# Elementwise arithmetic taken from GpSimd to VectorE and ScalarE in a two-layer attention, RWKV and experts trunk

## The chip, the cores and the metric

The kernel runs on one core of one Trainium2 chip. Such a core has a matrix engine (TensorE, PE in the profile; its weight loads are PEld), VectorE (DVE), ScalarE (ACT), GpSimd (POOL) and a queue that only issues transfers (SyncE, SP). Each engine takes its instructions strictly in the order in which they stand in its own queue. The metric is the time of one execution on the device in microseconds.

## The reference

Two layers over 1024 tokens of width 1024. The parts that the change touches are the projection, the RWKV half, the attention half and the output projection:

```python
for l in range(2):
    sh1, sc1, gt1, sh2, sc2, gt2 = split(silu(c) @ ada_w[l] + ada_b[l], 6)
    h = rms_norm(x, norm1_g[l]) * (1 + sc1) + sh1
    proj = h @ w_in[l]                                  # 1024 x 3232
    q, k, v = proj[:, :1536]                            # 4 heads, 2 maps of 64 each
    attn = diff_attention(rotary(q), rotary(k), v)      # softmax1 - lambda * softmax2, chunk mask
    p = proj[:, 1536:]; p = p + (shift(p) - p) * mu     # RWKV-7: 8 heads of 64
    r, k, v, w_lo, a_lo, g_lo = split(p)
    decay, a, g = exp(-exp(w)), sigmoid(a0 + a_lo @ a_up), sigmoid(g_lo) @ g_up
    kk = normalise(k * k_k); kf = k * (1 + (a - 1) * k_a)
    y = scan: S = S * w_t + (S a_t) b_t + v_t k_t;  y_t = S r_t
    rwkv = (head_group_norm(y) * lnx_g + lnx_b + sum(r * kf * r_k) * v) * g
    x = x + gt1 * (concat(attn, rwkv) @ w_out[l])
    h2 = rms_norm(x, norm2_g[l]) * (1 + sc2) + sh2
    x = x + gt2 * experts(h2)                           # 32 experts, top group, top 2
out = rms_norm(x, final_g)
```

All is float32. A product that must keep float32 accuracy is made of three faster ones: each factor is split into a high part (rounded to the matrix engine's narrower format, `fp32r`) and a low part, the difference between the value and its high part.

## The kernel before

Per layer there are three stages: the first norm (`norm1`), `phase_a` (projection, RWKV, attention, most of the output projection), and routing with the experts (`moe`).

**The weights of the input projection** come in 25 column blocks of 128 per layer. `split_w` (line 339) loads one (`wa_raw`), makes `wa_hi` by a copy (L346, on ScalarE but for the first two of a layer) and `wa_lo` by a subtraction (L347). There are two buffers each of hi and lo, so that a new `wa_hi` can be written only when the matrix engine is through with the block before last. `proj_cm` (L359 to L361) multiplies hi by hi, lo by hi and hi by lo.

**RWKV** goes by four pairs of heads (`hp`) and four quarters of the sequence (`q`), 256 tokens each. `rwkv_first` is called for each pair: `begin` makes two small products and their tanh (L641, L642), `chain` (lines 645 to 671) makes from them in some 13 VectorE instructions the tiles `arv`, `bk` and `bkb`; `bkb` is `bk` times `pend`, the decay at each chunk's end, and `arv[:, 0]` is a diagonal of `pend`. `products` multiplies them (`aa`) and masks them (`z`, L685), `turn` transposes `arv` and `bkb` on the matrix engine. The results go through memory in `sp_z` and `sp_av`. `solve` (L748, L750) inverts small triangles in 62 VectorE instructions for each pair.

`rwkv_second` takes these up again in 16 units of 256 tokens a layer: `rwkv_front` and `rwkv_mid` are products with small copies; `rwkv_back` carries the state from chunk to chunk: a product `rb_s` (L893), an addition on VectorE into `b_sb` (L895), and the next product that waits for it. Beside it stands the bonus `b_bo` (L879), a product of the read-out with one number per head; every second unit ends in `rwkv_last`, the norm of the read-out (L921 to L933) and the gate (L940).

**Attention** loads for each of 4 heads the two maps of keys and queries (`load_head`), makes hi by a ScalarE copy (L1091, L1096) and lo by a subtraction (L1092, L1097); the scores (L1171 to L1174), their maximum (L1176), the exponential (L1178), the difference of the two maps (L1185 to L1187), a transposition (L1196, L1197) and the product with the values (L1205) follow. `out_weights` makes hi and lo of the 8 blocks of the output projection (L1232 to L1234).

**The order.** `phase_a` is written as generators that `weave` interleaves by hand-set costs and lags. After that the framework's scheduler orders each engine's queue once more by its own estimate of times, so the place of an instruction in its queue moves with every change of engine.

Of the kernel before, what the change touches and what calls it, by code (L numbers as in the profile page):

```python
# [10 lines left out]
F32 = mybir.dt.float32  # L11
# [41 lines left out]
class Trunk:  # L53
# [285 lines left out]
    def split_w(self, wp, l, i, eng=None):  # L339

        nc = self.nc
        raw = wp.tile([128, NK, 128], F32, name="wa_raw", tag="wa_raw", bufs=1)
        nc.sync.dma_start(raw, self.a["w_in"][l, i])
        hi = wp.tile([128, NK, 128], F32R, name="wa_hi", tag="wa_hi")
        lo = wp.tile([128, NK, 128], F32R, name="wa_lo", tag="wa_lo")
        (eng or nc.vector.tensor_copy)(hi, raw)  # L346
        nc.gpsimd.tensor_tensor(lo, raw, hi.bitcast(F32), op=OP.subtract)  # L347
        return hi, lo


# [270 lines left out]
    def rwkv_first(self, hp, rp, ep, psum, krv, l2, w_up, a_up, sp):  # L621
# [22 lines left out]
        def chain(q):  # L644
            k, r, v = (x[:, H * q:H * q + H] for x in krv)
            kk = self.kn[:, H * q:H * q + H]
            th, ta = st["th"], st["ta"]
            P, u, rk = tl("P"), tl("u"), tl("rk")
            arv, bkb, bk = tl("arv", [128, 4, 4, 64]), tl("bkb", [128, 2, 4, 64]), tl("bk", [128, 2, 4, 64])
            nc.vector.tensor_scalar(th, th, 1.0, None, op0=OP.add)  # L650
            nc.vector.tensor_tensor_scan(u, self.smul, th, 0.0, op0=OP.mult, op1=OP.add)
            nc.scalar.activation(P, u, AF.Exp, scale=-0.5 * DECAY)
            nc.scalar.activation(u, u, AF.Exp, scale=0.5 * DECAY)

            nc.vector.tensor_scalar(ta, ta, -0.5, -0.5, op0=OP.mult, op1=OP.add)
            nc.vector.tensor_scalar(th, ta, self.nka[:, hp:hp + 1], self.omka[:, hp:hp + 1], op0=OP.mult, op1=OP.add)
            nc.vector.tensor_mul(th, th, k)
            nc.vector.tensor_mul(ta, ta, kk)
            nc.vector.scalar_tensor_tensor(rk, r, self.r_k[:, hp:hp + 1], th, op0=OP.mult, op1=OP.mult)
            kk3, P3 = v3(kk), v3(P)  # L660
            pend = P3[:, :, 63:64]
            nc.vector.tensor_mul(arv[:, 2, :, 1:64], kk3[:, :, 1:64], P3[:, :, 0:63])
            nc.scalar.copy(arv[:, 2, :, 0:1], kk3[:, :, 0:1])
            nc.vector.tensor_mul(arv[:, 1], v3(r), P3)
            nc.vector.tensor_mul(bk[:, 0], v3(ta), v3(u))
            nc.vector.tensor_mul(bk[:, 1], v3(th), v3(u))
            nc.scalar.copy(arv[:, 3], v3(v))
            for j in range(2):
                nc.gpsimd.tensor_tensor(bkb[:, j], bk[:, j], pend.to_broadcast([128, 4, 64]), op=OP.mult)
            nc.gpsimd.tensor_tensor(arv[:, 0], self.id2[:, None, :].to_broadcast([128, 4, 64]), pend.to_broadcast([128, 4, 64]), op=OP.mult)  # L670
            return arv, bkb, bk, rk

        def products(q, bk, arv, z):
# [190 lines left out]
    def rwkv_back(self, hp, q, t, pool, psum):  # L864
# [10 lines left out]
        if r == 0:  # L875
            self.bo = pool.tile([128, 4, 128], F32, name="b_bo", tag="b_bo")
            self.yh = pool.tile([128, 4, 128], F32, name="b_y", tag="b_y", bufs=2)
        bs = self.bsum[:, hp, 2 * q:2 * q + 2].rearrange("p t h -> p (t h)").unsqueeze(2).to_broadcast([128, 4, 64])
        nc.gpsimd.tensor_tensor(self.bo[:, r:r + 2].rearrange("p t (h n) -> p (t h) n", h=2), e[:, 1].rearrange("p t (h n) -> p (t h) n", h=2),  # L879
                                bs, op=OP.mult)  # L880
        hs = [slice(64 * h, 64 * h + 64) for h in range(2)]
        first = 0
# [33 lines left out]
    def rwkv_last(self, hp, half, y, bo, pool, psum):  # L916

        nc = self.nc
        y3 = y.rearrange("p t (h n) -> p (t h) n", h=2)
        st = pool.tile([128, 8, 2], F32, name="b_st", tag="b_st")  # L920
        nc.vector.tensor_reduce(st[:, :, 0:1], y3, axis=AX.X, op=OP.add)  # L921
        nc.vector.tensor_scalar(st[:, :, 0:1], st[:, :, 0:1], -1.0 / 64, None, op0=OP.mult)
        nc.vector.tensor_tensor(y3, y3, st[:, :, 0:1].to_broadcast([128, 8, 64]), op=OP.add)
        sq = pool.tile([128, 8, 64], F32, name="b_sq", tag="b_sq")
        nc.scalar.activation(sq, y3, AF.Square)
        nc.vector.tensor_reduce(st[:, :, 1:2], sq, axis=AX.X, op=OP.add)
        rs = self.rsqrt(pool, st[:, :, 1], 8, GN_EPS, 1.0 / 64, "gn")
        nc.vector.tensor_tensor(y3, y3, rs.unsqueeze(2).to_broadcast([128, 8, 64]), op=OP.mult)
        cs = slice(128 * hp, 128 * hp + 128)
        lnx = self.lnx  # L930
        nc.gpsimd.tensor_tensor(y, y, lnx[:, 0].unsqueeze(1).to_broadcast([128, 4, 128]), op=OP.mult)
        nc.gpsimd.tensor_tensor(bo, bo, lnx[:, 1].unsqueeze(1).to_broadcast([128, 4, 128]), op=OP.add)
        nc.gpsimd.tensor_tensor(y, y, bo, op=OP.add)  # L933

        def gate():
            ps = psum.tile([128, 4, 128], F32, name="rb_gt", tag="rb")
            for i in range(4):
                tl = 4 * half + i
                nc.tensor.matmul(ps[:, i, :], self.sg[0:96, 128 * tl:128 * tl + 128], self.g_up[0:96, cs], start=True, stop=True)
            nc.vector.tensor_mul(y, y, ps)  # L940
            nc.sync.dma_start(self.ad[half][:, :, 512 + 128 * hp:640 + 128 * hp], y)
            yield 0.85, 0.0

        self.add(3, gate(), self.clock + 12.0)
# [128 lines left out]
    def load_head(self, h):  # L1073


        nc, stage = self.nc, self.stage
        keep = self.stk[max(h - 1, 0)]
        qs, ks, kl = [], [], []
        halves = [slice(0, 64), slice(64, 128)]

        def tile(n, dt=F32R):
            return keep.tile([128, T], dt, name=f"at_{n}", tag=f"at_{n}")


        for j, m, x in ((1, 0, tile("q0", F32)), (1, 1, tile("q1", F32)), (0, 0, tile("v", F32)), (0, 1, stage.tile([128, T], F32, name="st", tag="st"))):
            for r in halves:
                nc.sync.dma_start(x[r], self.heads[h, j][halves[m]])
            if j:
                ks.append(tile(f"k{m}"))
                kl.append(tile(f"l{m}"))  # L1090
                nc.scalar.copy(ks[m], x)  # L1091
                nc.gpsimd.tensor_tensor(kl[m], x, ks[m].bitcast(F32), op=OP.subtract)  # L1092
            else:
                dst = tile(f"q{m}")
                qs.append(dst)
                nc.scalar.copy(dst, x)  # L1096
                nc.gpsimd.tensor_tensor(dst[64:128], x[64:128], dst[64:128].bitcast(F32), op=OP.subtract)  # L1097
        v = tile("v", F32).rearrange("p (t n) -> p t n", n=128)
        self.stacks[h] = (qs, ks, kl, v)
        nc.sync.dma_start(v, self.heads[h, 2])  # L1100
# [119 lines left out]
    def out_weights(self, l, k, wp, gate, keep):  # L1220
# [10 lines left out]
                      for n in names[2 * k:2 * k + 2])  # L1231
        nc.vector.tensor_tensor(raw, raw, gate, op=OP.mult)  # L1232
        nc.scalar.copy(hi, raw)
        nc.gpsimd.tensor_tensor(lo, raw, hi.bitcast(F32), op=OP.subtract)  # L1234
        self.wo[k] = hi, lo

    def open_output(self, l, x_src, side):
# [736 lines left out]
```

## Time and profile before

| | |
|---|---|
| median of 3 runs | 2728.67 us (2727.2 to 2737.83) |
| the profiled execution | 2742.43 us |
| its span | 2740.6 us |
| mean granted TensorE clock | 0.912 of full speed |
| GpSimd, busy | 711.9 us (26%), 525 instructions |
| VectorE, busy | 1836.7 us (67%) |
| ScalarE, busy | 1131.5 us (41%) |
| TensorE, busy | 2400.2 us (88%) |

Busy time of the matrix engine is modelled and contains waiting in its own pipe, so 88% is not 88% of its peak. In the span the first layer's first norm and its weights take up to about 150 us, its RWKV products to 450, the state's units beside the heads' projections to 760, attention with the output projection to 1000, the routing and experts to 1390; the second layer has the same stages from 1390, 1500, 1850, 2050 and 2300 us on.

### The profile page before, as it was taken

What the parts mean: (1) busy time and instruction counts of PE and PEld (TensorE: products, weight loads), DVE (VectorE), ACT (ScalarE), POOL (GpSimd) and SP (SyncE); (2) the same over time, 40 slices, a digit from 0 to 9 for tenths busy, and PEclk for the clock granted to TensorE, in tenths of its full rate; (3) what the DMA queues carried; (4) which work ended last, traced back from release to release, by engine and by line L of the source; (5) the groups of instructions that cost most, each with busy time, mean ns of one, the idle gap of its engine ahead of it and who ended that gap; (6) DMA issues with size and microseconds to landing.
All of it is one profiled execution on the core that took longest, in us unless ns stands there. A gap on an engine that the chain in (4) does not pass through costs nothing. (4 is left out here: it accounts for less than half of the span.)

```text
span 2740.6 us, 45306 instructions
## 1 busy us (share of the span) xinstructions
PE 2400.2 (88%) x17313; PEld 1836.5 (67%) x17313; DVE 1836.7 (67%) x3803; ACT 1131.5 (41%) x2020; POOL 711.9 (26%) x525
## 2 busy tenths in 40 slices
PE   5998989898979969999959888889986897999992
PEld 3676657687767866777737666667765786677771
DVE  3358875464658477877753689974648847787775
ACT  4333332244345225555544333324426422455552
POOL 4122221313141013333311222323314200233330
PEclk7999988798979979999979989889988897999996
DMA  8476675534272258999851434355426224899985
GB/s 286 159 233 222 177 218 155 155 115 132 88 218 70 96 193 303 355 336 368 309 213 47 155 107 150 113 153 156 136 76 204 73 89 180 303 384 352 335 311 200
DMA packets 262787, 542.68 MB, mean 198 GB/s; under 512 B 76376, under 2 KB 180768, under 8 KB 232608
## 3 DMA queue, kind: packets, MB, share of 16 engines
q1 hardware_dynamic: 234560, 484.61, 52.6%
q0 software_dynamic: 23376, 40.99, 4.0%
q10 hardware_dynamic: 4624, 14.06, 1.4%
q8 instruction: 142, 2.33, 0.4%
q14 instruction: 85, 0.70, 0.1%
HBM read 459.29 MB, written 120.09 MB: 211 GB/s over the span
## 5 line engine op out<-in xcount | busy, mean ns | idle before, releaser
L1618 DVE TENSOR_TENSOR w_lo<-w_gu,w_hi 128x2048 fp32r<-128x2048 f32 x134 | 306.4, 2287 | 69.1 <-ACT w_hi L1617 68.8
L1617 ACT CAST w_hi<-w_gu 128x2048 fp32r<-128x2048 f32 x134 | 255.7, 1908 | 211.0 <-PE h_ps L1670 204.3
L359 PE MATMUL pj<-hh,wa_hi 128*128 128x512 f32 x800 | 338.2, 423 | 2.1 <-DVE bsum L711 0.7
L361 PE MATMUL pj<-hh,wa_lo 128*128 128x512 f32 x800 | 328.1, 411 | 4.3 <-POOL wa_lo L347 4.3
L360 PE MATMUL pj<-hl,wa_hi 128*128 128x512 f32 x800 | 329.7, 412 | 1.2 <-DVE hl L336 1.1
L1698 POOL DMA_INDIRECT yd<-yo,idx_s x70 | 183.5, 2621 | 289.9 <-DVE yo L1695 275.1
L1709 PE MATMUL y_ps<-w_d,hT 128*128 128x512 f32 x560 | 252.3, 593 | 3.4 <-ACTq L1770 2.4
L1669 PE MATMUL h_ps<-w_hi,xT_hi 128*128 128x512 f32 x560 | 243.0, 434 | 4.4 <-ACT xT_hi L1653 4.4
L1670 PE MATMUL h_ps<-w_hi,xT_lo 128*128 128x512 f32 x560 | 222.5, 397 | 2.5 <-DVE xT_lo L1654 2.5
L1671 PE MATMUL h_ps<-w_lo,xT_hi 128*128 128x512 f32 x560 | 222.4, 397 | 0.0
L347 POOL TENSOR_TENSOR wa_lo<-wa_raw,wa_hi 128x1024 fp32r<-128x1024 f32 x50 | 123.4, 2468 | 296.2 <-ACT wa_hi L346 235.3
L359 PEld LDWEIGHTS pj<-hh,wa_hi 128*128 128x128 f32 x800 | 156.2, 195 | 42.9 <-issue 7.5
L361 PEld LDWEIGHTS pj<-hh,wa_lo 128*128 128x128 f32 x800 | 155.9, 195 | 41.1 <-POOL wa_lo L347 5.7
L360 PEld LDWEIGHTS pj<-hl,wa_hi 128*128 128x128 f32 x800 | 156.0, 195 | 37.1 <-DVE hl L336 4.4
L1709 PEld LDWEIGHTS y_ps<-w_d,hT 128*128 128x128 f32 x560 | 100.9, 190 | 104.8 <-issue 100.4
L1637 POOL DMA_INDIRECT xg<-h2d,idx_g x70 | 75.8, 1082 | 232.8 <-PE xT_ps L1645 204.2
L1669 PEld LDWEIGHTS h_ps<-w_hi,xT_hi 128*128 128x128 f32 x560 | 107.3, 192 | 38.0 <-issue 11.5
L1670 PEld LDWEIGHTS h_ps<-w_hi,xT_lo 128*128 128x128 f32 x560 | 107.3, 192 | 36.6 <-DVE th L1661 11.5
L1654 DVE TENSOR_TENSOR xT_lo<-xT_ps,xT_hi 128x1024 fp32r<-128x1024 f32 x70 | 85.7, 1225 | 65.6 <-ACT xT_hi L1653 65.6
L1671 PEld LDWEIGHTS h_ps<-w_lo,xT_hi 128*128 128x128 f32 x560 | 106.9, 191 | 23.0
L1178 ACT ACTIVATE at_p<-at_s,at_mx 128x256 f32<-128x256 f32 (+7 forms) x128 | 95.0, 743 | 64.4 <-DVE at_mx L1176 63.8
L748 DVE TENSOR_TENSOR sv_m<-sv_t,sv_n 64x31 f32<-64x31 f32 (+15 forms) x248 | 103.1, 416 | 26.4 <-DMA sv_n<-sp_z 21.8
(436 smaller groups left out, 5227.3 us busy)
## 6 DMA issues: line engine op xcount, KB each, us to landing
w_gu<-in_moe_w_gu SPq DMA_DIRECT2D x140, 1024.0 KB
w_d<-in_moe_w_down SPq DMA_DIRECT2D x70, 1024.0 KB
ada_w<-in_ada_w SPq DMA_DIRECT2D x80, 512.0 KB
wa_raw<-in_w_in SPq DMA_DIRECT2D x50, 512.0 KB
sp_z<-z SPq DMA_DIRECT2D x32, 768.0 KB
b_zz<-sp_z SPq DMA_DIRECT2D x32, 512.0 KB
cy<-yd SPq DMA_DIRECT2D x16, 1024.0 KB
qkv<-qst SPq DMA_DIRECT2D x48, 256.0 KB
```

The costliest lines, as they stand in the source:

```text
L347: nc.gpsimd.tensor_tensor(lo, raw, hi.bitcast(F32), op=OP.subtract)
L359: nc.tensor.matmul(ps, hi[:, k, :], self.hh[k][:, sl], start=(k == 0), stop=False)
L360: nc.tensor.matmul(ps, hi[:, k, :], self.hl[k][:, sl], start=False, stop=False)
L361: nc.tensor.matmul(ps, lo[:, k, :], self.hh[k][:, sl], start=False, stop=(k == NK - 1))
L748: eng.tensor_tensor(t3, tt[:, 0:j + 1, j].unsqueeze(2).to_broadcast([64, j + 1, 31 - j]), nt[:, j, j + 1:32].unsqueeze(1).to_broadcast([64 ...
L1617: self.nc.scalar.copy(hi, raw)
L1618: eng.tensor_tensor(lo, raw, hi.bitcast(F32), op=OP.subtract)
L1669: nc.tensor.matmul(ph, hi[:, k, :], whi[:, k % 4, :], start=(k == 0), stop=False)
L1670: nc.tensor.matmul(ph, lo[:, k, :], whi[:, k % 4, :], start=False, stop=False)
L1671: nc.tensor.matmul(ph, hi[:, k, :], wlo[:, k % 4, :], start=False, stop=(k == NK - 1))
L1698: st = nc.gpsimd.indirect_dma_start(out=self.yd, out_offset=bass.IndirectOffsetOnAxis(ap=self.idx_s[:, e:e + 1], axis=0), in_=yos[e % 2], ...
L1709: nc.tensor.matmul(po[:, 512 * half:512 * half + 512], hT[:, k, :], w[:, k, 512 * half:512 * half + 512], start=(k == 0), stop=(k == 1))
```

## The change

All tensor arithmetic that GpSimd does between the first norm and the experts is given to other engines. The subtractions L347, L1092, L1097 and L1234, the bonus L879 and the three operations of the read-out's norm (L931 to L933) go to VectorE with the same operands. The two products `bkb` and the diagonal `arv[:, 0]` (three instructions of 256 elements a partition for each quarter) become eight ScalarE copies with a scale taken from one column of `pend`: four of 128 elements and four of 64. GpSimd keeps its memory fills, its number patterns and the transfers it issues.

```diff
@@ split_w
-        nc.gpsimd.tensor_tensor(lo, raw, hi.bitcast(F32), op=OP.subtract)
+        nc.vector.tensor_tensor(lo, raw, hi.bitcast(F32), op=OP.subtract)
@@ rwkv_first, chain
-            for j in range(2):
-                nc.gpsimd.tensor_tensor(bkb[:, j], bk[:, j], pend.to_broadcast([128, 4, 64]), op=OP.mult)
-            nc.gpsimd.tensor_tensor(arv[:, 0], self.id2[:, None, :].to_broadcast([128, 4, 64]), pend.to_broadcast([128, 4, 64]), op=OP.mult)
+            for i in range(4):
+                nc.scalar.activation(bkb[:, :, i], bk[:, :, i], AF.Copy, scale=pend[:, i])
+            for i in range(4):
+                nc.scalar.activation(arv[:, 0, i], self.id2, AF.Copy, scale=pend[:, i])
@@ rwkv_back
-        nc.gpsimd.tensor_tensor(self.bo[:, r:r + 2]..., e[:, 1]..., bs, op=OP.mult)
+        nc.vector.tensor_tensor(self.bo[:, r:r + 2]..., e[:, 1]..., bs, op=OP.mult)
@@ rwkv_last
-        nc.gpsimd.tensor_tensor(y, y, lnx[:, 0]..., op=OP.mult)
-        nc.gpsimd.tensor_tensor(bo, bo, lnx[:, 1]..., op=OP.add)
-        nc.gpsimd.tensor_tensor(y, y, bo, op=OP.add)
+        nc.vector.tensor_tensor(y, y, lnx[:, 0]..., op=OP.mult)
+        nc.vector.tensor_tensor(bo, bo, lnx[:, 1]..., op=OP.add)
+        nc.vector.tensor_tensor(y, y, bo, op=OP.add)
@@ load_head
-                nc.gpsimd.tensor_tensor(kl[m], x, ks[m].bitcast(F32), op=OP.subtract)
+                nc.vector.tensor_tensor(kl[m], x, ks[m].bitcast(F32), op=OP.subtract)
-                nc.gpsimd.tensor_tensor(dst[64:128], x[64:128], dst[64:128].bitcast(F32), op=OP.subtract)
+                nc.vector.tensor_tensor(dst[64:128], x[64:128], dst[64:128].bitcast(F32), op=OP.subtract)
@@ out_weights
-        nc.gpsimd.tensor_tensor(lo, raw, hi.bitcast(F32), op=OP.subtract)
+        nc.vector.tensor_tensor(lo, raw, hi.bitcast(F32), op=OP.subtract)
```

The changed kernel has one line more in `chain`, so a line after it is numbered one higher (L895 is L896 there).

The queues move as follows. The first place is ScalarE's queue in the first layer's RWKV products, from one quarter's transposed tile `avt` to the next quarter's exponentials `P` and `u`; before:

```order
L693 COPY avt<-tp 128x512
L663 COPY arv<-kn 128x4
L667 COPY arv<-krv 128x256
L693 COPY z<-tp 128x512
L641 ACTIVATE th<-zwa,hbias_338 128x256
L642 ACTIVATE ta<-zwa,hbias_338 128x256
L652 ACTIVATE P<-u 128x256
L653 ACTIVATE u<-u 128x256
```

and in the changed kernel:

```order
L694 COPY avt<-tp 128x512
L663 COPY arv<-kn 128x4
L667 COPY arv<-krv 128x256
L671 ACTIVATE arv<-id_93,P 128x64 x4
L694 COPY z<-tp 128x512
L669 ACTIVATE bkb<-bk,P 128x2x64 x4
L641 ACTIVATE th<-zwa,hbias_338 128x256
L642 ACTIVATE ta<-zwa,hbias_338 128x256
L346 CAST wa_hi<-wa_raw 128x1024
L652 ACTIVATE P<-u 128x256
L653 ACTIVATE u<-u 128x256
```

The four copies of `bkb` now stand in front of the next quarter's tanh (L641), and those of the diagonal in front of the transposed `z`.

The second place is VectorE's queue in the same stage of the changed kernel, where `chain` (`th`, `ta`, `arv`, `bk`) and `solve` (`sv_m`, `sv_t`) are interleaved:

```order
L656 TENSOR_SCALAR th<-ta,ka_340 128x256
L749 TENSOR_TENSOR sv_m<-sv_t,sv_n 64x135
L347 TENSOR_TENSOR wa_lo<-wa_raw,wa_hi 128x1024
L657 TENSOR_TENSOR th<-th,krv 128x256
L658 TENSOR_TENSOR ta<-ta,kn 128x256
L751 TENSOR_TENSOR sv_t<-sv_t,sv_m 64x5x27
L377 SCALAR_TENSOR_TENSOR krv<-pj,pv_334,krv 128x511
L662 TENSOR_TENSOR arv<-kn,P 128x4x63
```

A weight's low part stands in the middle of a chain there, behind which the chain's other instructions have to wait for `wa_hi` too; before, that subtraction was in GpSimd's queue.

The third place is VectorE's queue where the state's units run (`b_sb`) and the first head's tiles for attention are made; before:

```order
L928 TENSOR_TENSOR b_y<-b_y,rs_y_gn 128x512
L821 COPY b_tt<-rb_t 32x4x32
L895 TENSOR_TENSOR b_sb<-rb_s,b_gg 64x64 x4
L838 COPY b_w<-rb_w 128x256
L895 TENSOR_TENSOR b_sb<-rb_s,b_gg 64x64 x2
```

and in the changed kernel:

```order
L929 TENSOR_TENSOR b_y<-b_y,rs_y_gn 128x512
L822 COPY b_tt<-rb_t 32x4x32
L932 TENSOR_TENSOR b_y<-b_y,b_lnx 128x512
L934 TENSOR_TENSOR b_y<-b_y,b_bo 128x512
L880 TENSOR_TENSOR b_bo<-b_e,bsum 128x256 x2
L933 TENSOR_TENSOR b_bo<-b_bo,b_lnx 128x512
L1093 TENSOR_TENSOR at_l_5728<-at_q_5721,at_k_5727 128x1024
L896 TENSOR_TENSOR b_sb<-rb_s,b_gg 64x64 x2
L1093 TENSOR_TENSOR at_l_5734<-at_q_5722,at_k_5733 128x1024
L896 TENSOR_TENSOR b_sb<-rb_s,b_gg 64x64 x2
L839 COPY b_w<-rb_w 128x256
L347 TENSOR_TENSOR wa_lo<-wa_raw,wa_hi 128x1024
```

Six moved instructions stand in front of a pair of state additions that followed at once before, and one more between that pair and the next.

## Rows read from the trace of the kernel before

**Rows 1.** Busy time by stage: span, PE, PEld, DVE, ACT, POOL (instructions), clock, DMA, GB/s.

```profile
150.00:450.00 300.00, 272.12 (x2345) 198.26 (x2346) 214.99 (x538) 98.98 (x200) 76.34 (x81) 0.91 0.69 212
450.00:760.00 310.00, 279.27 (x3301) 229.37 (x3300) 178.18 (x559) 108.32 (x280) 69.95 (x53) 0.88 0.41 119
760.00:1000.00 240.00, 210.94 (x1190) 179.55 (x1188) 163.26 (x383) 107.96 (x252) 46.82 (x28) 0.89 0.42 138
1500.00:1850.00 350.00, 306.15 (x2659) 235.45 (x2658) 278.91 (x740) 122.48 (x265) 90.00 (x81) 0.91 0.43 134
1850.00:2050.00 200.00, 185.60 (x2105) 151.25 (x2104) 98.85 (x312) 74.97 (x185) 56.68 (x40) 0.95 0.42 122
2050.00:2300.00 250.00, 209.83 (x1196) 179.50 (x1195) 176.39 (x396) 118.69 (x288) 46.17 (x26) 0.91 0.39 129
```

**Rows 2.** Timeline, one meeting of both engines: start us, us, engine, line, form.

```profile
372.80 2.95 POOL L347 TENSOR_TENSOR wa_lo<-wa_raw,wa_hi 128x1024 fp32r<-128x1024 f32 x1 [7.75 <-ACT wa_hi L346]
373.46 2.52 DVE L748 TENSOR_TENSOR sv_m<-sv_t,sv_n 64x220 f32<-64x220 f32 x1
376.78 0.37 DVE L750 TENSOR_TENSOR sv_t<-sv_t,sv_m 64x220 f32<-64x220 f32 x1
```

**Rows 3.** Timeline of DVE: the first and the last held instruction, with a neighbour.

```profile
34.98 2.34 DVE L108 TENSOR_TENSOR rs_u_n<-rs_u_n,rs_y_n 128x2 f32<-128x2 f32 x1
37.36 0.16 DVE L109 SCALAR_TENSOR_TENSOR rs_y_n<-rs_u_n,rs_y_n 128x2 f32<-128x2 f32 x1
...
2173.55 2.22 DVE L1212 SCALAR_TENSOR_TENSOR at_ob<-at_ob,rs_y_sub,subg 128x128 f32<-128x128 f32 x1
```

**Rows 4.** Timeline of PE: two waits, [idle us before, and what ended it].

```profile
239.23 1.14 PE L681 MATMUL aa<-arv,bk 64*64 64x128 f32 x14 [2.72 <-DVE arv L664]
...
2178.27 0.65 PE L1171 MATMUL at_s<-at_k,at_q 128*128 128x512 f32 x1 [2.49 <-ACT at_p L1178]
```

**Rows 5.** Groups of POOL, by form: count, busy us, mean ns, idle before, releasers.

```profile
L347 POOL TENSOR_TENSOR wa_lo<-wa_raw,wa_hi 128x1024 fp32r<-128x1024 f32 x50 | 123.4, 2468 | 296.2 <-ACT wa_hi L346 235.3 <-DVE sv_t L750 23.4 <-DVE rs_u_n L107 20.9
L669 POOL TENSOR_TENSOR bkb<-bk,P 128x256 f32<-128x256 f32 x64 | 44.7, 717 | 30.1 <-PE tp L692 14.4 <-DVE bk L666 11.9 <-DVE bk L665 2.8
L1092 POOL TENSOR_TENSOR at_l<-at_q,at_k 128x1024 fp32r<-128x1024 f32 x16 | 38.9, 2433 | 56.2 <-ACT at_k L1091 56.2
L670 POOL TENSOR_TENSOR arv<-id,P 128x256 f32<-128x256 f32 x32 | 28.6, 892 | 233.8 <-PE tp L692 138.1 <-ACT P L652 38.6 <-DVE sv_t L750 18.4
L931 POOL TENSOR_TENSOR b_y<-b_y,b_lnx 128x512 f32<-128x512 f32 x16 | 20.9, 1308 | 287.2 <-issue 182.1 <-DVE b_y L928 92.7 <-PE pj L360 9.1
```

**Rows 6.** Groups of DVE, by form: operations of the moved shapes.

```profile
L1791 DVE TENSOR_TENSOR cy<-cy 128x1024 f32<-128x1024 f32 x16 | 19.4, 1221 | 17.0 <-DMA cy<-yd 16.9
L665 DVE TENSOR_TENSOR bk<-ta,u 128x256 f32<-128x256 f32 x32 | 14.1, 441 | 0.2
L923 DVE TENSOR_TENSOR b_y<-b_y,b_st 128x512 f32<-128x512 f32 x16 | 11.1, 691 | 0.5
```

**Rows 7.** L347 alone in the two RWKV product stages: span, POOL busy (count), clock, DMA.

```profile
150.00:450.00 300.00, 28.42 (x12) 0.91 0.69 212
1500.00:1850.00 350.00, 34.38 (x13) 0.91 0.43 134
```

**Rows 8.** Waits over the whole span: who waited for whom, us, times, longest.

```profile
ACT wa_hi L346 <- PE pj L360: 93.0, 29, 9.3
POOL at_l L1092 <- ACT at_k L1091: 56.2, 10, 20.5
PE pj L361 <- POOL wa_lo L347: 4.3, 4, 1.5
```

**Rows 9.** Groups of ACT, by form: copies without and with a scale of one column.

```profile
L346 ACT CAST wa_hi<-wa_raw 128x1024 fp32r<-128x1024 f32 x46 | 48.1, 1047 | 106.8 <-PE pj L360 93.0 <-issue 7.1 <-DMA wa_raw<-in_w_in 3.7
L667 ACT COPY arv<-krv 128x256 f32<-128x256 f32 x32 | 13.1, 409 | 2.0 <-DVE krv L377 2.0
L323 ACT ACTIVATE n_y<-x,rs_y_n 128x1024 f32<-128x1024 f32 x8 | 8.7, 1139 | 0.6 <-DVE rs_y_n L109 0.6
L663 ACT COPY arv<-kn 128x4 f32<-128x4 f32 x32 | 6.5, 202 | 0.1
```

More of the change, by code (lines that the diff above doesn't have):

```diff
@@ L878, in rwkv_back @@
         bs = self.bsum[:, hp, 2 * q:2 * q + 2].rearrange("p t h -> p (t h)").unsqueeze(2).to_broadcast([128, 4, 64])
-        nc.gpsimd.tensor_tensor(self.bo[:, r:r + 2].rearrange("p t (h n) -> p (t h) n", h=2), e[:, 1].rearrange("p t (h n) -> p (t h) n", h=2),
+        nc.vector.tensor_tensor(self.bo[:, r:r + 2].rearrange("p t (h n) -> p (t h) n", h=2), e[:, 1].rearrange("p t (h n) -> p (t h) n", h=2),
                                 bs, op=OP.mult)
@@ L930, in rwkv_last @@
         lnx = self.lnx
-        nc.gpsimd.tensor_tensor(y, y, lnx[:, 0].unsqueeze(1).to_broadcast([128, 4, 128]), op=OP.mult)
-        nc.gpsimd.tensor_tensor(bo, bo, lnx[:, 1].unsqueeze(1).to_broadcast([128, 4, 128]), op=OP.add)
-        nc.gpsimd.tensor_tensor(y, y, bo, op=OP.add)
+        nc.vector.tensor_tensor(y, y, lnx[:, 0].unsqueeze(1).to_broadcast([128, 4, 128]), op=OP.mult)
+        nc.vector.tensor_tensor(bo, bo, lnx[:, 1].unsqueeze(1).to_broadcast([128, 4, 128]), op=OP.add)
+        nc.vector.tensor_tensor(y, y, bo, op=OP.add)
         def gate():
```

## The prediction

> **What bounds the kernel now.** I read the busy time by stage first, because the change leaves the experts alone: nothing moves in the two expert stages, about 390 and 440 us, and all of it lies in the six stages of [rows 1]. There the reader should compare the engines within a row. In the RWKV products (150 to 450 and 1500 to 1850 us) VectorE is busy for 215 of 300 and 279 of 350 us, 76% together, the fullest engine after a matrix engine whose busy time is modelled; ScalarE has 33 and 35%. Where the state's units run (450 to 760, 1850 to 2050) VectorE has 277 of 510 us, 54%; in attention (760 to 1000, 2050 to 2300) 340 of 490, 69%. So a VectorE instruction is dear in the first kind of stage and cheap in the second.
>
> Next I looked in the timeline for VectorE instructions that take far longer than their form. In [rows 2] one of 220 elements on 64 partitions takes 2.52 us, while the next of the same size takes 0.37. It starts 0.66 us after a GpSimd subtraction and ends 0.23 us after it (372.80 + 2.95 = 375.75; 373.46 + 2.52 = 375.98): it stood still while GpSimd worked. I compared every VectorE instruction that overlaps GpSimd tensor arithmetic with the median of its own form without overlap. 150 of them are held by over 0.1 us, 134 us in all; the first and the last are in [rows 3], a 128x2 operation of 2.34 us beside one of 0.16, and a 128x128 one of 2.22. By stage: 70 us in the RWKV products, 21 where the state's units run, 36 in attention, 7 in the first norms. The other way round GpSimd's instructions also vary, L670 averages 892 ns against 717 for L669 of the same size [rows 5].
>
> The Trainium skill, page "SBUF — State Buffer", section "Who interferes with whom", gives the rule: a VectorE instruction with two inputs in SBUF and a GpSimd instruction that reads SBUF exclude one another, and whichever begins first keeps the shared port until its end. By that rule all 134 us go with the arithmetic; by a mere sharing of bandwidth a held instruction would at most double, and the one in [rows 2] would have taken some 0.7 us. The trace agrees with the rule.
>
> Third, the matrix engine's waits. In these six stages I count its waits of over 0.4 us that no transfer ended: 151 us. 34 of them follow within 1.5 us of the end of a held VectorE instruction, and capping each wait at the time by which that instruction was held gives 51 us: 18 in the RWKV products, 9 where the state's units run, 24 in attention. The first and the last are in [rows 4]. This, not 134, is the most that the removed stalls give back at once.
>
> **The change part by part.**
>
> Removed: GpSimd's tensor operations and VectorE's 134 us behind them.
>
> Added to VectorE: the shapes of 1024 elements, 50 + 16 + 16 + 16 = 98 instructions (input weights, keys, queries, output weights), at 1.221 us [rows 6] are 119.7 us; 32 of 256 at 0.441 are 14.1; 48 of 512 at 0.691 are 33.2. That is 167 us against 134, so VectorE's busy time rises by 33 us. What matters is where. In the RWKV products stand 25 weight subtractions [rows 7], and by the same count 8 of the bonus and 8 of the read-out: 30.5 + 3.5 + 5.5 = 39.5 us against 70 removed, 31 less on the fullest engine. Where the state's units run 68 us come in against 21, 48 more; in attention 42 against 36, 6 more; in the norms 17 against 7.
>
> *RWKV products.* I take 18 us: nearly the whole of the waits behind held instructions, since VectorE's load falls there as well. Bounds: 31 (all that VectorE sheds) and 0 (the matrix engine finds other waits).
>
> *State units.* 9 us of waits go. Against that 48 us net stand on VectorE, in part directly ahead of state additions, as the third place in the order shows: six instructions of 0.69 to 1.22 us, some 5 us, ahead of one pair. VectorE has 46% free here, and the scheduler fills the matrix engine with projections. I charge 10 us, a fifth of the addition. Result: 1 us lost; bounds 9 gained (all hidden) and 39 lost (all 48 on the path).
>
> *Attention.* 24 us of waits go, 42 us of VectorE work come in, which can be laid where no score waits, while the holds hit whatever stood next. GpSimd needed 2.43 us for a low part [rows 5], VectorE half of it, so the stacks are complete earlier. I charge 16 of the 42: 8 us gained; bounds 24 gained and 18 lost.
>
> *Low parts of the input weights.* One is ready 1.2 us sooner (2.468 to 1.221); the matrix engine waited for it 4.3 us in all [rows 8]. I take 2; bounds 0 and 4.
>
> *Scaled copies on ScalarE.* No row shows one of 64 or 128 elements from SBUF with a scale. From below, a plain copy of 4 elements takes 202 ns; from above, one of 256 takes 409, and a scale of one column adds 92 (1139 against 1047 at 1024 elements): 0.50 us [rows 9]. The slope between 256 and 1024 elements is 0.83 ns each, which puts 128 at 0.396 and 64 at 0.343; I take these. 128 of each make 95 us (52 to 129), ScalarE going from some 34 to 49% in those stages, which hides them. A quarter needs 4 x 0.396 + 4 x 0.343 = 2.96 us instead of 2 x 0.717 + 0.892 = 2.33 on GpSimd [rows 5, 9], 0.63 more, 20 us over 32 quarters; and the tanh of the next quarter stands behind four of them, as the first place in the order shows. But that tanh overwrites a tile that this quarter's `bk` still reads, so it waited for nearly as long before. I charge 3; bounds 0 and 20.
>
> Sum: 18 - 1 + 8 + 2 - 3 = 24 us. The profiled execution took 2742.4 us, so 2718. The median of the runs shown is 13.8 us below it, and all times here are given against that median: 2728.7 - 24 = **2705 us**.
>
> **The rivals.**
>
> *More is won: the clock too.* The granted clock in [rows 1] is 0.88 to 0.95. A mean of 0.91 over two levels, 1.2 and 2.4 GHz, means 18% of the time at the lower. The six stages lose 0.09 x 300 + 0.12 x 310 + 0.11 x 240 + 0.09 x 350 + 0.05 x 200 + 0.09 x 250 = 155 us to it. If fewer waits take away a fifth of that, 31 us come on top: 2674. For it: the clock is below full in all six stages, and the matrix engine waits in all six. Against it: two thirds of its waits stay.
>
> *Nothing is won.* The 24 us come back as added work in the state's units and in attention, 58 us of it charged at 50 instead of 26: 2729. For it speaks that VectorE's total rises, against it that its free time lies in just these stages.
>
> *It gets slower: the low parts block VectorE's queue.* On GpSimd a subtraction could wait for its high part at no cost. ScalarE itself stood for 93 us in 29 waits before `wa_hi` until the matrix engine freed the buffer, and the keys' low parts waited 56 us [rows 8]. On VectorE the chain, the state additions and the maxima stand behind them, as the second place in the order shows, and the matrix engine waits for those in turn. If VectorE stands for half of 149 us, and four fifths of that is on the path, 60 us are lost against 24 won: 2765. It decides from 30 us of such waiting on. Against it: in the RWKV products VectorE is behind the others, so it would reach the subtraction late, and the scheduler places it late.
>
> *The holds are not GpSimd's.* Then VectorE bears 167 us more. [Rows 2] speaks so clearly that I give it no chance of its own; it would end like the slower case.
>
> **How the numbers follow.** Chances: the forecast 0.44, more won 0.19, nothing won 0.19, slower 0.18. A reordering of all queues shifts a time by itself, so the forecast's own range is wide, 2685 to 2715. The range of 8 in 10 reaches from 2655, past the clock's case by the forecast's own spread, to 2755, into the blocked queue's case. About 0.5%, 13.6 us, is what a measurement of this kernel can tell from no change. Faster than 2715.0 are the forecast and the clock's case, 0.63; within 0.5% the case of nothing won, 0.19; slower than 2742.3 the blocked queue, 0.18.
>
> **What would show it.** In the profile after, GpSimd's busy time in the six stages should fall to almost nothing, and operations such as L750 at 64x220 and the 128x1 product L1186 should have one duration each, without values over 2 us. VectorE's busy time should be about 1870 us, ScalarE's about 1226. The scaled copies should take 0.34 to 0.40 us. The stages of RWKV products should shorten, together by 15 to 30 us, attention by a little, and the state's units stay within some 10 us. I am wrong if waits of VectorE for `wa_hi` or `at_k` add up to over 30 us, if the state's units grow by over 20 us, or if the matrix engine's waits for `z`, `arv` and `bk` stay as they were though the holds are gone.

## The result and the profile after

The changed kernel takes 2694.42 us (median of 4 runs, 2688.92 to 2695.11) against 2731.43 of before on the same chip: ratio 0.9858, 95% interval 0.9833 to 0.9884, so 37 us or 1.4% faster. 2705 us were forecast. The two profiled spans, 2740.6 and 2693.3 us, differ by 47, because the profiled execution of before was one of its longer ones.

The page's line of busy times, engine by engine, in the changed kernel:

```profile
PE 2378.4 (88%) x17313; PEld 1824.6 (68%) x17313; DVE 1845.3 (69%) x3981; ACT 1194.5 (44%) x2276; POOL 313.3 (12%) x251
```

GpSimd lost 399 of 712 us. VectorE took over 98 + 80 instructions and is busy only 9 us longer than before (1836.7). The groups by form of the changed kernel say why: first three operations that had been held, then what was added (count | busy us, mean ns | idle before):

```profile
L1187 DVE SCALAR_TENSOR_TENSOR at_g<-at_sum,nlam,at_rec 128x1 f32<-128x1 f32 x64 | 13.8, 216 | 0.9
L1213 DVE SCALAR_TENSOR_TENSOR at_ob<-at_ob,rs_y_sub,subg 128x128 f32<-128x128 f32 x64 | 18.3, 346 | 0.4
L108 DVE TENSOR_TENSOR rs_u_n<-rs_u_n,rs_y_n 128x2 f32<-128x2 f32 x20 | 3.2, 160 | 0.6
...
L347 DVE TENSOR_TENSOR wa_lo<-wa_raw,wa_hi 128x1024 fp32r<-128x1024 f32 x50 | 61.0, 1221 | 44.9 <-ACT wa_hi L346 44.3 <-DMA b_aa<-sp_z 0.2
L932 DVE TENSOR_TENSOR b_y<-b_y,b_lnx 128x512 f32<-128x512 f32 x16 | 11.0, 689 | 0.4
L669 ACT ACTIVATE bkb<-bk,P 128x128 f32<-128x128 f32 x128 | 40.9, 396 | 2.1 <-DVE bk L665 2.1
L671 ACT ACTIVATE arv<-id,P 128x64 f32<-128x64 f32 x128 | 34.1, 339 | 0.0
```

The same three operations before:

```profile
L1186 DVE SCALAR_TENSOR_TENSOR at_g<-at_sum,nlam,at_rec 128x1 f32<-128x1 f32 x64 | 28.5, 446 | 1.3
L1212 DVE SCALAR_TENSOR_TENSOR at_ob<-at_ob,rs_y_sub,subg 128x128 f32<-128x128 f32 x64 | 24.5, 441 | 0.4
L108 DVE TENSOR_TENSOR rs_u_n<-rs_u_n,rs_y_n 128x2 f32<-128x2 f32 x20 | 5.4, 269 | 0.6
```

A hold is the time by which a VectorE instruction outlasts its form's median while GpSimd computes. No VectorE instruction overlaps GpSimd arithmetic any more, and the 134 us of holds [rows 2, 3] are gone: L1187 now takes between 0.208 and 0.222 us, L751 at 64x220 between 0.352 and 0.380. The scaled copies take 0.396 and 0.339 us. They stand back to back and overlap: 128 of 396 ns are only 40.9 us busy.

Where the time went is read by stage. I cut both traces at the same events, not at round times: first product `aa`, last `rb_y`, last `po`. Per layer that gives one stretch with the RWKV products and the state's units, which overlap in the second layer, and one with attention. The windows of before and then of the changed kernel, columns as in [rows 1], in the order RWKV, attention, of the first and then the second layer:

```profile
155.90:764.70 608.80, 549.78 (x5675) 426.28 (x5674) 388.45 (x1087) 206.22 (x477) 144.54 (x130) 0.90 0.54 163
...
764.70:982.20 217.50, 194.71 (x1073) 164.97 (x1068) 147.97 (x328) 100.54 (x242) 44.91 (x26) 0.91 0.41 134
...
1513.30:2047.10 533.80, 475.55 (x4689) 374.37 (x4690) 366.07 (x1031) 189.49 (x435) 142.15 (x117) 0.92 0.44 131
...
2047.10:2290.20 243.10, 204.22 (x1170) 173.80 (x1165) 171.23 (x369) 114.11 (x283) 46.17 (x26) 0.92 0.38 122
```

```profile
159.60:759.30 599.70, 542.96 (x5631) 422.68 (x5629) 392.75 (x1154) 236.57 (x599) 11.28 (x26) 0.91 0.54 164
...
759.30:966.00 206.70, 187.65 (x1075) 162.12 (x1071) 149.68 (x346) 100.33 (x242) 1.66 (x3) 0.93 0.44 141
...
1499.00:2022.80 523.80, 473.36 (x4685) 373.47 (x4686) 369.02 (x1090) 219.33 (x554) 4.77 (x14) 0.93 0.44 133
...
2022.80:2243.50 220.70, 198.59 (x1169) 169.82 (x1165) 163.83 (x387) 113.19 (x283) 1.69 (x3) 0.95 0.41 134
```

RWKV went from 1142.6 to 1123.5 us (19 less; split at the last transposition `tp`, the products give 24 and the state's units take 5 back). Attention went from 460.6 to 427.4, 33 less, where I had forecast 8. What lies ahead of the two RWKV stretches grew by 4 and 2, the rest is unchanged within 1. Some 10 us of the 47 are the longer execution of before, and nothing shows in which stage they lie. In attention the part of the window in which the matrix engine is not busy fell from 61.7 to 41.2 us, and its busy time from 398.9 to 386.2 for the same products at a higher granted clock (0.91 and 0.92 to 0.93 and 0.95): 20.5 us of waits and 12.7 us of clock (busy time times clock is 365 us before and 363 after).

The waits of the whole span in the changed kernel (who waited for whom: us, times, longest):

```profile
ACT wa_hi L346 <- PE pj L360: 79.5, 30, 12.7
...
DVE wa_lo L347 <- ACT wa_hi L346: 44.3, 17, 5.9
...
DVE at_l L1093 <- ACT at_k L1092: 13.1, 8, 3.3
...
DVE at_q L1098 <- ACT at_q L1097: 8.5, 4, 3.7
...
PE pj L361 <- DVE wa_lo L347: 3.6, 2, 3.1
```

VectorE does stand for its new work, for 66 us. The matrix engine's wait for `wa_lo` hardly moved (4.3 to 3.6) [rows 8]. Its waits for the chain's tiles `z`, `arv` and `bk` before, and then in the changed kernel, where VectorE's `arv` is gone from the list:

```profile
PE tp L692 <- DVE z L685: 7.4, 7, 2.7
...
PE aa L681 <- DVE arv L664: 6.7, 3, 2.7
...
PE aa L681 <- DVE bk L665: 2.8, 2, 2.3
```

```profile
PE tp L693 <- DVE z L686: 5.4, 3, 3.8
...
PE aa L682 <- DVE bk L665: 1.3, 1, 1.3
```

### The profile page after: what moved, and what is told of

The parts are those of the page before. It is cut to its first block, busy times and chain, and to the rows that moved or that the text cites. A ratio compares the mean times of both kernels' runs of the same rounds, so it can differ in the third digit from the quotient of the medians.

```text
span 2693.3 us, 45292 instructions
## 1 busy us (share of the span) xinstructions
PE 2378.4 (88%) x17313; PEld 1824.6 (68%) x17313; DVE 1845.3 (69%) x3981; ACT 1194.5 (44%) x2276; POOL 313.3 (12%) x251
## 4 chain that ended last, share of the span: by engine, by line
PE 41%; issue 19%; DMA 14%; DVE 12%; POOL 9%; ACT 3%; SPq 1%; POOLq 0%; DVEq 0%; ACTq 0%
POOL yd L1699 6%; PE pj L359 5%; PE pj L360 5%; PE pj L361 5%; DMA ada_w<-in_ada_w 3%; POOL xg L1638 2%; PE po L1309 2%; PE po L1311 2%; PE po L1310 2%; PE at_o L1206 2%; DMA sp_z<-z 2%; PE ada_ps L238 2%; DMA yd<-yo,idx_s 2%; PE rb_y L909 1%; DMA cy<-yd 1%
## 5 line engine op out<-in xcount | busy, mean ns | idle before, releaser
L1696 DVE SCALAR_TENSOR_TENSOR yo<-y_ps,wsl,gt 128x1024 f32<-128x1024 f32 x70 | 89.9, 1284 | 38.3 <-PE y_ps L1710 38.3
L238 PE MATMUL ada_ps<-ada_w,crep 128*32 128x128 f32 x1536 | 71.3, 312 | 44.1 <-DMA ada_w<-in_ada_w 43.8
L1177 DVE TENSOR_REDUCE at_mx<-at_s 128x1 f32<-128x256 f32 (+7 forms) x128 | 95.7, 753 | 20.3 <-PE at_s L1175 19.1
```

The source lines that it names most:

```text
L238: nc.tensor.matmul(ps[32 * j:32 * j + 32, :], self.crep[:, nk * q + i, :], w[:, i, j * 128:(j + 1) * 128], start=(q + i == 0), stop=(q == ...
L1177: nc.vector.tensor_reduce(mx, ps[:, 0:n], axis=AX.X, op=OP.max, negate=True)
```

## The experiments

Two theories were to be told apart. *Holds*: VectorE is faster because GpSimd's reads no longer stop it. *Order*: each change of engine rearranges all queues, and earlier low parts or a luckier order gave the gain. Every ratio is against the kernel before. The first four make one part of the change alone.

**Attention's low parts alone.**

```diff
-                nc.gpsimd.tensor_tensor(kl[m], x, ks[m].bitcast(F32), op=OP.subtract)
+                nc.vector.tensor_tensor(kl[m], x, ks[m].bitcast(F32), op=OP.subtract)
```
and the same for the queries (L1097) and the output weights (L1234).

> The kernel before with only attention's part of the change: the keys', queries' and output weights' low parts (L1092, L1097, L1234) on VectorE. In the kernel before these three lines stand behind 43 of VectorE's 134 us of holds, most of them L1234 (27). After the whole change the two attention stages were 33 us shorter, where I had put 8. Theory A (holds): these stalls stood where scores wait, so this part alone gives nearly the whole of it: 20 to 35 us faster, that is 2696 to 2711, all of it in attention. Rival B (the forecast's balance: 42 us of added VectorE work eat most of what the holds give): 0 to 12 us faster. Rival C (the gain in attention is the queues' new order, which the other parts of the change bring): within 7 us of before, of either sign, with the 43 us of holds gone all the same.

Measured: 2702.92 us, ratio 0.9893 (0.9862 to 0.9924), 29 us faster. The two attention windows, columns as above:

```profile
747.10:954.40 207.30, 186.20 (x1072) 159.65 (x1068) 148.15 (x344) 100.18 (x242) 5.04 (x10) 0.94 0.44 141
2031.30:2252.70 221.40, 198.50 (x1169) 169.71 (x1164) 162.54 (x385) 113.19 (x283) 5.04 (x10) 0.95 0.41 134
```

428.7 us, as in the whole change (427.4), clock included. Theory A: the gain in attention belongs to this part, and the 39 us of low parts that VectorE now makes in these windows cost nothing that can be seen. VectorE's busy time in the windows even fell, from 319.2 to 310.7. In RWKV the first layer became 18 us shorter and the second 12 longer. A third of the moved instructions (8 a layer) run there, in the state's units; the products, where no instruction of this edit runs, became 8 us shorter in the first layer and 6 longer in the second: that much comes of the queues' new order without an edit in the stage.

**Input weights' low parts alone.**

```diff
-        nc.gpsimd.tensor_tensor(lo, raw, hi.bitcast(F32), op=OP.subtract)
+        nc.vector.tensor_tensor(lo, raw, hi.bitcast(F32), op=OP.subtract)
         return hi, lo
```

> The kernel before with only the low parts of the input weights (L347) on VectorE. They stand behind 51 us of holds, most in the RWKV products; 50 subtractions of 1.22 us (61 us) come onto VectorE. Theory A (holds): the products' stages shorten by 8 to 20 us together, the total by as much (2711 to 2723). Rival B (only load counts): 10 us more on VectorE, so 0 to 10 us slower. Rival C (the blocked queue of the forecast): VectorE waits over 30 us for the high parts and the total is 10 us or more above before; the profile tells by VectorE's waits for wa_hi.

Measured: 2729.58, ratio 0.9981 (0.9966 to 0.9996), 5 us faster. In its profile, taken of its longest execution (2740.2 us), the RWKV stretches are 13 us shorter, attention, which has no edit here, 8 longer. Less than theory A, on its side of zero. The waiting that rival C named came, 44.5 us of VectorE for `wa_hi`, but not its loss.

**The chain's products as ScalarE copies alone.** The edit is that of the change in `chain`.

> The kernel before with only the products of the chain's keys and the diagonal as eight scaled ScalarE copies a quarter (128 of 64 and 128 of 128 elements). The three GpSimd products stand behind 26 us of holds. Theory A (holds): products' stages 4 to 10 us shorter, since each quarter takes 0.3 to 0.6 us longer on ScalarE than on GpSimd but VectorE is free of the holds. Rival B (latency): the longer chain decides, 32 x 0.6 = 19 us slower at most, 5 or more. The copies should take 0.34 to 0.40 us by the forecast.

Measured: 2730.58, ratio 1.0000 (0.9986 to 1.0014). RWKV is 12 us shorter in the profile, the total is not. Neither theory's size came; the copies took the forecast's times.

**Bonus and read-out alone.**

```diff
-        nc.gpsimd.tensor_tensor(self.bo[...], e[:, 1]..., bs, op=OP.mult)
+        nc.vector.tensor_tensor(self.bo[...], e[:, 1]..., bs, op=OP.mult)
-        nc.gpsimd.tensor_tensor(y, y, lnx[:, 0]..., op=OP.mult)
+        nc.vector.tensor_tensor(y, y, lnx[:, 0]..., op=OP.mult)
```
and the other two of the read-out.

> The kernel before with only the bonus (L879) and the read-out's three operations (L931 to L933) on VectorE. They stand behind 15 us of holds, 80 instructions and 47 us come onto VectorE among the state additions. The whole change lengthened the state's units by 5 us. Theory A: this is the part that loses: 2 to 8 us slower, in the state's units, with longer waits of the matrix engine for b_sb. Rival B (holds): 3 to 8 us faster, the holds there being on the path of the state.

Measured: 2754.68, ratio 1.0087 (1.0059 to 1.0115), 24 us slower, three times what theory A allowed. In its profile the first layer's state units are 17 us longer, the other stages shift by up to 10 either way. Both layers' state units together are 6 us longer and the span 8 (2748.7 against 2740.6), so the profile doesn't place the 24 us. The matrix engine's wait for `b_sb` before `rb_s`, which theory A named, stayed as it was (10.4 before, 10.6 here). This part works against the rest, by a path that isn't shown.

**Holds brought back without dependents, and a control.** To the changed kernel a GpSimd subtraction is added behind each of the 98 low parts; in the control, fills instead (`cut` gives a view of the raw tile's first elements).

```diff
         nc.vector.tensor_tensor(lo, raw, hi.bitcast(F32), op=OP.subtract)
+        nc.gpsimd.tensor_tensor(raw, raw, hi.bitcast(F32), op=OP.subtract)
```
```diff
         nc.vector.tensor_tensor(lo, raw, hi.bitcast(F32), op=OP.subtract)
+        nc.gpsimd.memset(self.cut(raw, 1024, False), 0.0)
+        nc.gpsimd.memset(self.cut(raw, 1024, False), 0.0)
+        nc.gpsimd.memset(self.cut(raw, 512, False), 0.0)
```

> The changed kernel, in which VectorE keeps all its new work, and behind each of the 98 low parts (L347, the keys', the queries', the output weights') a GpSimd subtraction of the same tiles, whose result overwrites the raw tile that is dead by then; nobody reads it. It brings back GpSimd's reads of SBUF (some 220 us of subtractions) without any step that waits for their result. Theory A (holds): VectorE's instructions are held again, by 70 to 110 us, and the time rises over that of the next run, the control, by 25 to 45 us, 20 to 33 of it in attention. Rival C (order and earlier low parts gave the gain, the holds are harmless): within 8 us of the control.

> Control for the run before: the changed kernel with three GpSimd memory fills (1024, 1024 and 512 elements, about 2.4 us together) of the dead raw tile at each of the same 98 places. GpSimd is as busy and the raw tile comes free as late, but it reads nothing from SBUF. Theory A (holds need GpSimd's reads): no VectorE instruction over 0.3 us too long, and the time within 8 us of the changed kernel (2686 to 2703). Rival D (any work on GpSimd, or the raw tiles' late release, costs the time): 20 us or more above the changed kernel, as in the run before.

Measured: 2776.72, ratio 1.0165 (1.0126 to 1.0205), with the subtractions; 2686.36, ratio 0.9827 (0.9800 to 0.9855), with the fills. 0.0338 apart, 92 us, over twice the 25 to 45 that I expected, with GpSimd equally busy (560.8 and 550.9 us). Counted as for the prediction, 120 us of holds are back with the subtractions (70 in RWKV, 40 in attention; expected were 70 to 110). The fills hold none of these instructions, though some others, against my expectation of none over 0.3 us (last section). The attention windows of the first and then of the control:

```profile
778.90:1007.70 228.80, 195.60 (x1076) 165.60 (x1072) 170.89 (x346) 102.06 (x243) 44.65 (x24) 0.90 0.40 128
2078.00:2326.50 248.50, 209.52 (x1170) 176.86 (x1165) 190.26 (x387) 114.07 (x283) 44.18 (x24) 0.90 0.38 119
```

```profile
757.30:966.10 208.80, 188.24 (x1072) 161.33 (x1068) 150.35 (x346) 100.29 (x242) 40.87 (x56) 0.93 0.44 140
2017.30:2240.90 223.60, 200.93 (x1169) 171.53 (x1165) 164.79 (x387) 113.67 (x283) 40.68 (x56) 0.95 0.42 133
```

477.3 against 432.4 us: nobody reads what these subtractions write, and still attention is 45 us longer, 29 of it waits of the matrix engine and 16 its busy time at a clock of 0.90. RWKV is 40 us longer (1161.2 against 1121.1). A later release of the raw tiles isn't the reason: in attention the waits of the three other engines for a transfer or for GpSimd add up to 18 us with the subtractions and 20 with the fills. The timeline of the first shows a single meeting (start us, us):

```profile
2092.69 1.22 DVE L1236 TENSOR_TENSOR wo_raw<-wo_raw,gt 128x1024 f32<-128x1024 f32 x1
2092.92 3.20 POOL L1239 TENSOR_TENSOR wo_raw<-wo_raw,wo_hi 128x1024 f32<-128x1024 f32 x1 [66.59 <-DVE wo_lo L1238]
2093.83 3.38 DVE L1238 TENSOR_TENSOR wo_lo<-wo_raw,wo_hi 128x1024 fp32r<-128x1024 f32 x1
```

GpSimd's 2.39 us last 3.20, since VectorE's L1236 runs until 2093.91; then L1238, 1.22 us when free, lasts 3.38, until GpSimd ends at 2096.12 and for 1.1 us more. In this meeting each stops the other until its own end. In attention this decides for the holds.

**Parts taken back from the changed kernel**, one in each run, and one run with all low parts on VectorE but chain and read-out as before. The edits are the diff's hunks in reverse.

> The changed kernel with the bonus and the read-out's three operations (L880, L932 to L934 there) back on GpSimd, the rest as changed. Alone, their move to VectorE cost 24 us. Theory A (that loss is theirs, by 47 us of VectorE work ahead of the state additions): 15 to 25 us faster than the changed kernel, about 2674, in the state's units above all. Rival C (the loss there was a chance of the queues' order): within 8 us of the changed kernel, of either sign. Rival H (holds): 5 us slower or more, since 15 us of holds come back.

> The kernel before with all the low parts (L347, L1092, L1097, L1234) on VectorE, and the chain's products and the read-out left on GpSimd. The two parts alone gave 29 and 5 us. If parts add up: 34 us faster, 2699. If the parts meet (with both gone, GpSimd is left with short operations only, and 95 of 134 us of holds are gone): more than 40 us faster. If the queues' order decides: anything between 20 and 34.

> The changed kernel with the chain's three products back on GpSimd, the rest as changed. Alone, from the kernel before, this part was worth nothing (ratio 1.000); between all low parts and the same with this part (two runs above, 2714 and 2675) lie 38 us. Theory A (holds): 26 us of holds come back, 8 to 20 us slower than the changed kernel, in the RWKV products. Rival I (parts meet: once GpSimd has little else to do, this is the part that counts): 25 us slower or more. Rival C (order): within 8 us of the changed kernel.

> The changed kernel with the input weights' low parts (L347) back on GpSimd. Alone this part gave 5 us. Theory A (holds): some 50 us of holds come back, 10 to 25 us slower than the changed kernel, products and state's units alike. Rival B (load): VectorE sheds 61 us of work, which makes up for the holds, so within 8 us of the changed kernel or faster.

> The changed kernel with attention's low parts (keys, queries, output weights) back on GpSimd. Alone this part gave 29 us. Theory A (holds in attention): 25 to 35 us slower than the changed kernel, some 30 of it in the two attention stages. Rival C (order): less than 15 us slower.

> The changed kernel with only the read-out's three operations (L932 to L934, 33 us of VectorE work) back on GpSimd; the bonus (14 us) stays on VectorE. With both back it was 2675, 19 us under the changed kernel. Theory A (work ahead of the state additions decides, so by the work moved): two thirds of it, 10 to 15 us faster than the changed kernel, 2680 to 2685. Rival B (the bonus stands nearest to the state's additions and carries most of the loss): within 6 us of the changed kernel.

Measured, with the sums of both layers from each profile (stretches as above) and VectorE's holds in them, counted as for the prediction:

| kernel | median us | ratio (interval) | RWKV us | attention us | holds RWKV / attention |
|---|---|---|---|---|---|
| changed | 2694.42 | 0.9858 (0.9833 to 0.9884) | 1123.5 | 427.4 | 0 / 0 |
| read-out and bonus back | 2675.42 | 0.9804 (0.9774 to 0.9834) | 1103.4 | 430.0 | 18 / 0 |
| read-out back | 2695.25 | 0.9863 (0.9843 to 0.9883) | 1124.2 | 429.7 | 9 / 0 |
| chain back | 2706.72 | 0.9904 (0.9881 to 0.9928) | 1137.4 | 426.7 | 25 / 0 |
| weights back | 2725.84 | 0.9964 (0.9947 to 0.9982) | 1162.4 | 428.2 | 56 / 0 |
| attention back | 2723.01 | 0.9956 (0.9941 to 0.9972) | 1122.6 | 457.4 | 14 / 38 |
| low parts only | 2713.63 | 0.9933 (0.9907 to 0.9960) | 1144.3 | 429.6 | 41 / 0 |

By the difference of ratios times 2731, the parts are worth in the changed kernel: attention 27 us, weights 29, chain 13, read-out with bonus minus 15. Alone they were worth 29, 5, 0 and minus 24.

*Attention* adds up: theory A both times. Over all 14 profiles its two stretches take 429 us plus 0.97 us for each microsecond of hold in them (correlation 0.97, worked out from their windows). These are two groups, eight profiles without holds there and six with 31 to 40 us, so the line says what a group costs and not that it is straight between them.

*Weights*: 5 us alone, 29 at the end, theory A's side there and above its 10 to 25. With L347 back on GpSimd, VectorE has 61 us of work less, 43 of it in RWKV, and yet is busier in RWKV than in the changed kernel; the windows of that run:

```profile
154.60:768.30 613.70, 550.10 (x5667) 425.10 (x5668) 400.95 (x1132) 237.47 (x597) 55.51 (x44) 0.90 0.54 161
1504.80:2053.50 548.70, 486.59 (x4691) 383.57 (x4690) 381.92 (x1078) 220.93 (x555) 47.87 (x32) 0.90 0.42 128
```

783 us here, 762 in the changed kernel: 56 us of holds came back for 43 us of work that left.

*Chain*: 13, as theory A had it, at the end (the two intervals overlap a little); nothing alone. The low parts without the chain's change gave 18 us, fewer than attention alone and not the 34 of a sum; all three together 53 (the row with read-out and bonus back). RWKV is not additive. Why the chain's part counts only in company is not settled.

*Read-out*: taking back the bonus and the read-out gains 15 us (theory A's bound; the two intervals touch) and makes the fastest kernel of all, 2675.42 us. In that run RWKV takes 20 us less than in the changed kernel, all of it in the state's units; VectorE has 44 us of work less there (L880 and L932 to L934) for 18 us of holds:

```profile
161.40:747.30 585.90, 535.34 (x5631) 418.91 (x5629) 381.00 (x1116) 237.42 (x599) 52.00 (x59) 0.92 0.56 168
1481.60:1999.10 517.50, 475.44 (x4685) 373.56 (x4686) 357.43 (x1052) 220.14 (x554) 46.52 (x47) 0.93 0.45 135
```

Taking back the read-out without the bonus gains nothing, which is what rival B said and theory A didn't. The path that theory A named isn't it: the matrix engine's wait for `b_sb` before `rb_s` is 16.1 us with both back and 15.0 in the changed kernel. Whether the bonus itself is the dear part, or the order that this edit brought, these runs don't tell: order moved a layer's RWKV products by 8 us in the first run, where no edit stood.

## Why the prediction was right, and where not

*The holds are GpSimd's, and the arithmetic's removal ends them*: right. L1186 (L1187 in the changed kernel) fell from 446 to 216 ns, and adding reads back brought them, and the time, back. The matrix engine's waits for `z`, `arv` and `bk` fell from 16.9 to 6.7 us.

*RWKV products, 18 us; state's units, minus 1; low parts 2; scaled copies minus 3*: 16 us together, 19 measured. The products gave 24 and the state's units lost 5. But the sum agrees better than its terms: alone, the weights gave 5 and the copies cost nothing, while the read-out and bonus cost 24 alone and 15 at the end. I had charged 10 us for the whole 48 us of work in the state's units. Read-out and bonus together belonged at a higher price there, and the other parts paid for it: that 16 met 19 is in part luck. The path that I gave for this loss, instructions ahead of the state additions, isn't borne out, since the waits for `b_sb` are as long without them. Nor do the six instructions that I put at some 5 us take so long: two of them are of 0.44 us, and the six together make 4.2.

*Attention, 8 us*: this is the step that failed in size, 33 instead of 8, outside its bound of 24. Two things in it were wrong. First "I charge 16 of the 42": the added work cost nothing visible. ScalarE's wait for the maximum, which stands behind VectorE's queue, shrank by more than half, where I had expected the low parts to delay it. In the second layer's attention before, and after:

```profile
ACT at_p L1178 <- DVE at_mx L1176: 28.7, 19, 5.6
```

```profile
ACT at_p L1179 <- DVE at_mx L1177: 12.6, 11, 3.7
```

Second, the bound of 24 held only the matrix engine's waits. These did fall by 20.5 us, near the 24; the other 12.7 are the same products at a higher clock. I had put the clock into a rival with no part of it in the forecast, though it moved with the same waits: in the attention windows of all runs with holds there the clock is 0.90 to 0.93, without them 0.93 to 0.96.

*More is won, the clock too (2674)*: its mechanism is real, its size smaller. The mean granted clock rose from 0.912 to 0.920, and the matrix engine's busy time fell by 22 us over the span (2400.2 to 2378.4), where the rival had 31.

*Nothing is won*: for the read-out it holds, for the whole it doesn't. The 58 us in it is a slip: what I had charged at 26 is 48 and 42, so 90 us of work.

*The low parts block VectorE's queue*: the waiting came, 44.3 us for `wa_hi` and 21.6 for the keys and queries. That is above the 30 us from which I called myself wrong, and it cost nothing that shows: with the input weights' low parts alone the wait for `wa_hi` is as long, 44.5 us, and that kernel is 5 us faster, not slower. What the wait costs beside the holds that go with it, no run separates. The criterion was bad. A wait counts only where what stands behind it is late for the matrix engine, and VectorE has 31% of the span free.

*Busy times*: VectorE 1845 instead of 1870. The added instructions are as long as forecast (1.221 and 0.689 us), 166 us together, and those that both kernels have shed 142, little more than the 134 that I counted. That makes 24 us; the busy time rose by 9, because neighbouring instructions overlap and it counts an overlap once. ScalarE 1195 instead of 1226 for the same reason: its instructions became 92 us longer in sum, near the forecast 95, and its busy time 63.

## What to carry to other kernels

Count the instructions that last far longer than their form's median and see what another engine does meanwhile; moving that work onto the held engine can leave it hardly busier (here 9 us for 166 us of work), because a small operation can be held for 2 us. In a stage where the matrix engine waits for such an engine, price a hold at its whole length and let the clock gain with the waits, as both did here in attention; price added work by what stands behind it, not by its sum. Where a change has several parts, try each alone and each taken back: here one part cost 15 to 24 us, and the kernel without it is the faster one.

## What the runs showed of the hardware that was not expected

GpSimd's fills hold VectorE too, but other instructions of it. In the control none of the operations with two tile inputs was long, but forms with one were: L658 and L663 (0.287 and 0.283 us in the changed kernel, where they are L650 and L655) took up to 1.1 us, and in all 27 instructions, nearly all TENSOR_SCALAR and COPY, were held for 12.6 us. From its timeline:

```profile
171.30 0.60 DVE L658 TENSOR_SCALAR th<-th 128x256 f32<-128x256 f32 x1
171.81 0.98 POOL L354 MEMSET wa_raw<- 128x1024 f32 x1
171.82 1.12 DVE L663 TENSOR_SCALAR ta<-ta 128x256 f32<-128x256 f32 x1
...
2104.17 0.96 POOL L1250 MEMSET wo_raw<- 128x1024 f32 x1 [3.38 <-DVE wo_1at_k L1249]
2104.53 1.15 DVE L1202 SCALAR_TENSOR_TENSOR at_p<-at_p,at_g,at_p 128x896 f32<-128x896 f32 x1
```

L663 starts 0.01 us after the fill and ends 0.15 us after it (172.94 and 172.79). L1202, with two tiles of input, takes 1.15 us beside a fill, and the mean of that form in the changed kernel is 1.148. The Trainium skill, page "SBUF — State Buffer", section "Who interferes with whom", has both cases: `tensor_scalar` and copies can enter a mode that takes both ports and then contend with GpSimd, and two inputs contend with its reads only. The trace agrees. The Trainium skill, page "ScalarE: Activation LUTs", section "What ACT_TABLE_LOAD costs", gives an activation 186 ns and 0.833 ns an element, 93 ns more for a scale taken from a column, and an overlap of 93 ns between neighbours. An estimate by that page is 332 and 386 ns for the scaled copies; measured are 339 and 396. 128 of 396 ns are 50.7 us in sum and 40.9 busy; of the 128 copies 96 follow directly on one of their own four, so these overlap by 101 ns each, and those of the diagonal by 98.
